# A transformer trunk in split fp32: the hi weight multiplies the hi and the lo half of an activation in one 512-column matmul, and the two partial sums are added when PSUM is read out

## The chip, the cores and the metric

The kernel runs on one core of one Trainium2 chip. The metric is device time in microseconds; three executions of the kernel before took 1297.39 to 1297.92 us, with a median of 1297.69 us.

## The reference

Two layers of a pre-norm residual network work on 256 tokens of width 1024 (float32), followed by a last RMSNorm. Cut to its matrix products, a layer is:

```python
# per layer; h is (256, 1024)
u = rms_norm(h, norm_mix_g)
q, k, v, g_ret, c_in, gates = split(u @ w_in)          # six parts: 1024, 1024, 2048, 2048, 2048, 2048 wide
y_a = (silu(g_ret) * group_norm(chunk_retention(rotary(q), rotary(k), v))) @ w_ret_out   # 2048 -> 1024
a, b = split(c_in)
y_b = silu(layer_norm(causal_dwconv(a * sigmoid(b), width=31))) @ w_conv_out + b_conv_out
g_a, g_b = split(sigmoid(gates + b_gate))
h = h + (g_a * y_a + g_b * y_b) @ w_mix_out
# cross-attention, 4 heads, into a memory of 256 tokens
kx, vx = split(rms_norm(mem, norm_mem_g) @ w_xkv)
h = h + softmax_attention(rms_norm(h, norm_xattn_g) @ w_xq, kx, vx) @ w_xo
# gated MLP, 1024 -> 2 x 2816 -> 1024
val, gate = split(rms_norm(h, norm_ffn_g) @ w_up)
h = h + (silu(causal_dwconv(gate, width=3)) * val) @ w_down
```

## The kernel before

**Split products.** Every weight and every activation of a projection is held as two tiles of the type fp32r: a hi part (a rounded copy) and a lo part (the value less its hi part). A product is the sum of three matmuls: hi weight on hi activation, hi weight on lo activation, lo weight on hi activation. The function `feat` (L166 to L174) issues these three for each 128 rows k of the contraction, with a 128x128 weight tile as the stationary operand and the 256 tokens as 256 moving columns. All three add up in the same 256 columns of a PSUM bank. `both` (L265) does the same for two output tiles in turn, so that the first k of both come before the last k of either. `tok` (L176) is the other way round, with the activation stationary and 512 weight columns moving, and serves the value and gate parts of the input projection and the values of the memory.

**Steps and weights.** The program is a list of steps, built in order by `mixer`, `cross` and `ffn` for each layer. Most steps are one chunk of 256 output features, that is two units of weights, one for each 128 features. `run` (L136) walks the list and, ahead of each step, emits the preparation of weight units up to four beyond those done (`UNITS`): `fetch` loads 1 MB by a DMA on SyncE's queue into one of four raw tiles, then `prepare` (L126) makes the hi part by a ScalarE copy (L131) and the lo part by a VectorE subtraction (L132). A list scheduler of the compiler orders each engine's instructions by priority and by when their inputs are ready; functions marked `urgent` (the residuals and the norms of h) have a higher priority.

**Buffers.** Activations of the size 1024 x 256 live in ten equal SBUF blocks (`BLOCKS`), which are handed out by whichever is free; a hi/lo pair takes two of them. Sums take a PSUM bank of 2 x 256 columns each; four such banks (tag `mm`) turn round for the projections, three (tag `att`) for attention, one (tag `nrm`) for norms. Small temporaries of 2 x 256 columns come from eight slots (`TEMPS`).

**Evictions.** What reads a projection's bank differs by stage: `split` (L161) writes hi on ScalarE (L163) and lo on VectorE (L164); `residual` (L334) adds the bank to h (L336), adds squares to the running sum of the next norm (`ssq_add`) and, where asked, writes an early copy of h times the norm's gain, split in hi and lo (`gained`, L252); conv_out adds a bias and multiplies by a gate (L704), then adds to the tile `m` (L708); the FFN's gate copies the bank on ScalarE first (L838), its value part multiplies out of the bank (L855).

**Order of the stages in a layer.** Input projection (conv parts, then per head queries, keys, values, gates, then the two mixing gates), ret_out (eight steps of 16 k each, L652), conv_out (four steps, L696), the first of four key steps of the memory (`mem_k`, L448), mix_out (four steps), three more key steps, during which h is normed for attention; then queries, attention with the values of the memory in between, xo (four steps, the first by `both`), the FFN's up projection in 22 steps and down projection in eight steps of 22 k each. The first four steps of the input projection and of the up projection run on the early copy (`ahead`, L293) while the norm's scale is worked out. The norm of the memory (`memory`, L434) loads the memory by a DMA on SyncE's queue (L438), sums its squares, and writes a normed hi/lo pair (`normed`, L321); it stands behind the seventh step of ret_out (`MEM_AT` = 6, L664). All matmuls are in TensorE's one queue, and so are the small matmuls that sum and spread a norm (L203, L211).

Of the kernel before, what the change touches and what calls it, by code (L numbers as in the profile page):

```python
# [13 lines left out]
P = 128  # L14
D = 1024
KT = 8
# [28 lines left out]
BLOCKS = 10  # L45
# [3 lines left out]
MEM_AT = 6  # L49


def by_token(x):
    return x.rearrange("p k n -> p (k n)").rearrange("p (t d) -> p t d", t=2)

# [9 lines left out]
class Trunk:  # L64
    def __init__(self, ctx, tc, io):
# [12 lines left out]
        self.background = []  # L78

# [4 lines left out]

    def block(self, dt=F32, tag="blk", bufs=BLOCKS):
        return self.bp.tile([P, KT, N], dt, name=self.nm(tag), tag=tag, bufs=bufs)
# [6 lines left out]

    def bank(self, tag="mm", bufs=4):
        return self.pp.tile([P, 2, N], F32, name=self.nm(tag), tag=tag, bufs=bufs)
# [79 lines left out]

    def tok(self, outs, ws, u, half):  # L176
# [13 lines left out]
    def flat_banks(self):  # L190
        return [self.bank().rearrange("p t n -> p (t n)") for _ in range(2)]
# [49 lines left out]
    def begin(self, gain=None):  # L241


        def fn():
            self.ssq, self.gain = None, gain
            if gain == "final":
                self.out = self.block()
            elif gain:
                self.early = self.block(F32R), self.block(F32R)
        self.step(fn)  # L250

    def gained(self, k, n):  # L252
# [68 lines left out]
    def normed(self, h, rstd, gname, layer):  # L321
        nc = self.nc
        uh, ul = self.block(F32R), self.block(F32R)
        for j in range(KT // 2):
# [5 lines left out]
            self.split(u, uh[:, 2 * j:2 * j + 2, :], ul[:, 2 * j:2 * j + 2, :])  # L330
        return uh, ul

    @urgent
    def residual(self, ps, k, n=2):  # L334
        h = self.h[:, k:k + n, :]
        self.nc.vector.tensor_tensor(h, ps, h, op=ALU.add)  # L336
# [97 lines left out]
    def memory(self, layer):  # L434
# [10 lines left out]
        self.xk = self.block(F32R), self.block(F32R)  # L445
        self.xv = self.block(F32R), self.block(F32R)

    def mem_k(self, layer, c, midway=None):  # L448
        def fn(*w):
            ps, pr = self.bank(), slice(2 * c, 2 * c + 2)  # L450
            self.each(ps, w, self.mem, midway)
            self.split(ps, self.xk[0][:, pr, :], self.xk[1][:, pr, :])
        self.step(fn, *self.pair("w_xkv", layer, c))

    def mem_v(self, layer, c):

        def fn(*w):
            if c % 2 == 0:
# [9 lines left out]
    def mixer(self, layer):  # L468
# [5 lines left out]
        def alloc_conv():  # L474
            X["c"], X["cc"] = self.block(), self.block()
# [95 lines left out]
        def gate(h):  # L571
# [5 lines left out]
            hi, lo = X["y"]  # L577
            b, r = h // 2, (h % 2) * 4
# [435 lines left out]
```

## Time and profile before

| What | Value |
|---|---|
| Median of three executions | 1297.69 us |
| Profiled execution, its own time | 1297.52 us |
| Its span, first to last instruction | 1295.7 us |
| Granted TensorE clock, mean | 0.997 |
| TensorE matmuls | 9632, busy 1278.4 us (99%) |
| VectorE | 1283 instructions, busy 972.8 us (75%) |
| ScalarE | 1365 instructions, busy 857.7 us (66%) |
| GpSimd | 31 instructions, busy 27.9 us (2%) |
| DMA | 227.32 MB, mean 175 GB/s |

A busy share is the part of the span in which an engine had an instruction in work. Matmuls overlap: the next starts before the last has ended, so the mean duration of one is a latency and the sum over a group is not a time that the group takes. PE in a row of the profile is TensorE's matmuls, PEld its loads of stationary operands, DVE is VectorE, ACT ScalarE, SP SyncE. A row's L number is a line of the kernel printed above. The idle time at a row's end is that of the engine ahead of the group's instructions, with what ended it behind an arrow.

### The profile page before, as it was taken

Reading aid. Unit: us, or ns where it says so; the run is one execution under the profiler, and the core shown is the slowest. Engines: PE = TensorE matmul, PEld = TensorE weight load, DVE = VectorE, ACT = ScalarE, POOL = GpSimd, SP = SyncE. Lnnn points to the kernel's source line nnn. Section 1 sums busy time; section 2 is a strip of 40 time slices with the busy share of each in tenths; the row PEclk is TensorE's granted clock in tenths of the full one; section 3 lists DMA queues with packets and bytes.
Section 4 is the critical chain, followed back from the end, with each engine's and each line's share of the span. In section 5 each row is a group of like instructions: output and inputs, shape, how many; then the busy total and the mean of one; then the engine's idle time right before and its main releaser. Section 6 shows DMA issues by size and latency. Waiting matters only on the chain.

```text
span 1295.7 us, 23296 instructions
## 1 busy us (share of the span) xinstructions
PE 1278.4 (99%) x9632; PEld 1225.2 (95%) x9632; DVE 972.8 (75%) x1283; ACT 857.7 (66%) x1365; POOL 27.9 (2%) x31
## 2 busy tenths in 40 slices
PE   7999999999999999999999999999999999999997
PEld 7998888999999999999999888899999989999997
DVE  8989998767676688665677999985686766876653
ACT  6899999664445557664469899986454554666542
POOL 0000000000000000000000010000000000000000
PEclk9999999999999999999999999999999999999998
DMA  8554444555554445544555444444654544455450
GB/s 306 208 180 163 163 158 169 193 187 194 178 190 137 157 168 192 190 163 181 189 190 183 170 158 172 163 165 162 228 190 172 176 147 163 169 189 189 156 178 33
DMA packets 33082, 227.32 MB, mean 175 GB/s; under 512 B 3920, under 2 KB 4176, under 8 KB 6736
## 3 DMA queue, kind: packets, MB, share of 16 engines
q1 hardware_dynamic: 32688, 225.32, 49.4%
q8 instruction: 75, 1.23, 0.4%
q10 hardware_dynamic: 288, 0.52, 0.1%
q14 instruction: 31, 0.25, 0.1%
HBM read 224.78 MB, written 1.05 MB: 174 GB/s over the span
## 4 chain that ended last, share of the span: by engine, by line
PE 84%; issue 14%; DMA 0%; DVE 0%; ACT 0%; SPq 0%; POOLq 0%; POOL 0%; DVEq 0%
PE mm L172 20%; PE mm L173 20%; PE mm L174 20%; PE mm L185 17%; PE mm L274 3%; PE att L553 1%; PE att L745 1%; PE att L746 1%; PE att L744 1%; PE att L575 1%; PE att L542 1%; PE att L555 1%; PE nrm L211 0%; DMA raw<-in_w_in_dram 0%; PE nrm L203 0%
## 5 line engine op out<-in xcount | busy, mean ns | idle before, releaser
L172 PE MATMUL mm<-blk,whi 128*128 128x256 f32 x2624 | 745.4, 285 | 0.0
L173 PE MATMUL mm<-blk,whi 128*128 128x256 f32 x2624 | 742.3, 283 | 0.0
L174 PE MATMUL mm<-blk,wlo 128*128 128x256 f32 x2624 | 742.2, 283 | 0.0
L131 ACT ACTIVATE whi<-raw 128x1024 fp32r<-128x1024 f32 (+1 forms) x424 | 443.2, 1050 | 346.4 <-PE mm L173 270.7
L132 DVE TENSOR_TENSOR wlo<-raw,whi 128x1024 fp32r<-128x1024 f32 (+1 forms) x424 | 511.0, 1211 | 193.8 <-ACT whi L131 191.9
L172 PEld LDWEIGHTS mm<-blk,whi 128*128 128x128 f32 x2624 | 502.8, 192 | 2.6 <-issue 1.7
L173 PEld LDWEIGHTS mm<-blk,whi 128*128 128x128 f32 x2624 | 503.0, 192 | 2.3 <-issue 2.2
L174 PEld LDWEIGHTS mm<-blk,wlo 128*128 128x128 f32 x2624 | 502.9, 192 | 0.3 <-issue 0.2
L185 PE MATMUL mm<-whi,blk 128*128 128x512 f32 x640 | 201.9, 391 | 0.0
L499 ACT ACTIVATE prod<-blk,params 128x255 f32<-128x255 f32 (+14 forms) x480 | 197.2, 487 | 3.8 <-DVE blk L502 3.8
L502 DVE TENSOR_TENSOR blk<-blk,prod 128x1020 f32<-128x1020 f32 (+14 forms) x120 | 138.2, 1151 | 7.9 <-ACT prod L499 6.8
L185 PEld LDWEIGHTS mm<-whi,blk 128*128 128x128 f32 x640 | 119.6, 188 | 25.1 <-issue 1.2
L185 PE MATMUL mm<-wlo,blk 128*128 128x512 f32 x320 | 128.2, 401 | 0.0
L185 PEld LDWEIGHTS mm<-wlo,blk 128*128 128x128 f32 x320 | 60.1, 188 | 12.8 <-issue 0.7
L163 ACT ACTIVATE blk<-t 128x512 fp32r<-128x512 f32 (+1 forms) x71 | 42.5, 614 | 16.1 <-DVE t L261 12.4
L164 DVE TENSOR_TENSOR blk<-t,blk 128x512 fp32r<-128x512 f32 (+1 forms) x71 | 47.0, 676 | 2.6 <-ACT blk L163 2.6
L274 PE MATMUL mm<-blk,whi 128*128 128x256 f32 x192 | 39.7, 295 | 7.9 <-ACT whi L131 7.9
L274 PEld LDWEIGHTS mm<-blk,whi 128*128 128x128 f32 x192 | 32.5, 201 | 7.9 <-ACT whi L131 7.9
L848 DVE SCALAR_TENSOR_TENSOR t<-t,params,t 128x255 f32<-128x255 f32 (+1 forms) x88 | 38.2, 478 | 0.0
L336 DVE TENSOR_TENSOR h<-mm,h 128x512 f32<-128x512 f32 (+1 forms) x26 | 16.9, 650 | 20.9 <-PE mm L174 16.0
L274 PE MATMUL mm<-blk,wlo 128*128 128x256 f32 x96 | 28.3, 295 | 1.1 <-DVE wlo L132 1.1
L218 POOL TENSOR_TENSOR rs_r<-rs_m,mhalf 128x2 f32<-128x2 f32 x11 | 8.5, 777 | 888.5 <-DVE rs_m L217 888.5
(133 smaller groups left out, 742.4 us busy)
## 6 DMA issues: line engine op xcount, KB each, us to landing
raw<-in_w_in_dram SPq DMA_DIRECT2D x79, 1024.0 KB, 4.9
raw<-in_w_up_dram SPq DMA_DIRECT2D x44, 1024.0 KB, 4.9
raw<-in_w_ret_out_dram SPq DMA_DIRECT2D x16, 1024.0 KB, 4.9
raw<-in_w_xkv_dram SPq DMA_DIRECT2D x16, 1024.0 KB, 4.9
raw<-in_w_down_dram SPq DMA_DIRECT2D x16, 1024.0 KB, 5.0
raw<-in_w_conv_out_dram SPq DMA_DIRECT2D x8, 1024.0 KB, 5.8
raw<-in_w_mix_out_dram SPq DMA_DIRECT2D x8, 1024.0 KB, 4.8
raw<-in_w_xq_dram SPq DMA_DIRECT2D x8, 1024.0 KB, 4.8
```

Of the source, the lines that this page charges most:

```text
L131: nc.scalar.activation(hi[:, :n], raw, AF.Copy)
L132: nc.vector.tensor_tensor(lo[:, :n], raw, hi[:, :n].bitcast(F32), op=ALU.subtract)
L163: self.nc.scalar.activation(hi, src, AF.Copy)
L164: self.nc.vector.tensor_tensor(lo, src, hi.bitcast(F32), op=ALU.subtract)
L172: self.nc.tensor.matmul(out, wh[:, k, :], uh[:, k0 + k, :], start=a, stop=False)
L173: self.nc.tensor.matmul(out, wh[:, k, :], ul[:, k0 + k, :], start=False, stop=False)
L174: self.nc.tensor.matmul(out, wl[:, k, :], uh[:, k0 + k, :], start=False, stop=b)
L185: mm = lambda a, b, p, q: self.nc.tensor.matmul(out, a[:, k, ts], b[:, j, :], start=p, stop=q)
L274: mm = lambda x, y, a, b: self.nc.tensor.matmul(out, x[:, k, :], y[:, k, :], start=a, stop=b, skip_group_check=True)
L499: nc.scalar.activation(t[:, i, :m], X["c"][:, k, :m], AF.Copy, scale=self.par("conv_dw_w", L, k * TAPS + TAPS - 1 - s))
L502: nc.vector.tensor_tensor(cc, cc, t[:, :, :m], op=ALU.add)
L848: nc.vector.scalar_tensor_tensor(g[:, f, s:], x[:, f, :N - s], wt(k, 2 - s), g[:, f, s:], op0=ALU.mult, op1=ALU.add)
```

## The change

A hi/lo pair becomes one tile with the two halves beside each other (`blocks`, `halved`, `Split`); there are five such pairs for the ten blocks. For every projection outside the input projection (and outside the first four up steps, which stay in `ahead`), `wide` streams hi and lo past the hi weight in one matmul of 2 x 256 columns, and then hi past the lo weight in one of 256 columns, which adds to the first 256. The 2 x 256 columns fill a bank, so a step with two output tiles takes two banks: `banks` hands out a pair of banks, of which there are two, and `bank` now hands out the halves of such a pair in turn. `add_up` copies the second sums to SBUF on ScalarE and adds the first on VectorE; `residual` adds both to h one after the other. `gained` writes the hi half by a scaled ScalarE copy and the lo half by one fused VectorE operation. The first xo step no longer uses `both`. In ret_out the product with the gate is written over the gate, and the tile `m` is gone. `memory` moves from behind the seventh step of ret_out to behind the first step of conv_out, and the tiles for the memory's values, for attention's output and for the FFN's activations are taken only where they are first written.

```diff
-BLOCKS = 10
+BLOCKS = 5
-MEM_AT = 6
+MEM_AT = 0
+    def blocks(self, dt=F32):
+        return self.bp.tile([P, 2, KT, N], dt, name=self.nm("blk"), tag="blk", bufs=BLOCKS)
+    def banks(self):
+        self.spare = None
+        return self.pp.tile([P, 2, 2, N], F32, name=self.nm("mm"), tag="mm", bufs=2)
...
+    def wide(self, ps, w, u, first=True, last=True):
+        kt = w[0].shape[1]
+        for k in range(kt):
+            self.nc.tensor.matmul(ps, w[0][:, k, :], u.tile[:, :, k, :], start=first and k == 0, stop=False)
+            self.nc.tensor.matmul(ps[:, 0, :], w[1][:, k, :], u[0][:, k, :], start=False, stop=last and k == kt - 1)
+
+    def wides(self, w, u):
+        pair = self.banks()
+        for f, x in enumerate(w):
+            self.wide(pair[:, f], x, u)
+        return pair
+
+    def add_up(self, pair):
+        t = self.temp()
+        self.nc.scalar.activation(t, pair[:, :, 1, :], AF.Copy)
+        self.nc.vector.tensor_tensor(t, pair[:, :, 0, :], t, op=ALU.add)
+        return t
...
-            t, pr = self.temp(), slice(k, k + n)
-            for i in range(n):
-                nc.vector.tensor_scalar(t[:, i, :], self.h[:, k + i, :], self.par(*self.gain, k + i), None,
-                                        op0=ALU.mult)
-            self.split(t[:, :n, :], self.early[0][:, pr, :], self.early[1][:, pr, :])
+            for i in range(k, k + n):
+                hi, lo = (x[:, i, :] for x in self.early)
+                g = self.par(*self.gain, i)
+                nc.scalar.activation(hi, self.h[:, i, :], AF.Copy, scale=g)
+                nc.vector.scalar_tensor_tensor(lo, self.h[:, i, :], g, hi.bitcast(F32), op0=ALU.mult,
+                                               op1=ALU.subtract)
...
-        self.nc.vector.tensor_tensor(h, ps, h, op=ALU.add)
+        for j in range(2):
+            self.nc.vector.tensor_tensor(h, pair[:, :, j, :], h, op=ALU.add)
...
-            self.each(ps, w, self.mem, midway)
-            self.split(ps, self.xk[0][:, pr, :], self.xk[1][:, pr, :])
+            for f in range(2):
+                self.wide(pair[:, f], w[f], self.mem)
+                if midway and f == 0:
+                    midway()
+            self.split(self.add_up(pair), self.xk[0][:, pr, :], self.xk[1][:, pr, :])
...
-            if f == MEM_AT:
-                self.step(lambda: self.memory(L))
...
             self.step(fn, *self.pair("w_conv_out", L, j))
+            if j == MEM_AT:
+                self.step(lambda: self.memory(L))
...
-                ps = self.bank()
-                (self.each if j else self.both)(ps, w, X["o"])
-                self.residual(ps, 2 * j)
+                self.residual(self.wides(w, X["o"]), 2 * j)
...
-                    self.feat(X["ps"][:, at, :], w[b], X["a"][b], first=b == 0, last=b == 2)
+                    self.wide(X["ps"][:, f % 2], w[b], X["a"][b], first=b == 0, last=b == 2)
```

More of the change, by code (lines that the diff above doesn't have):

```diff
@@ L83, in nm, with block, halved @@
         return f"{s}_{self.uid}"
-    def block(self, dt=F32, tag="blk", bufs=BLOCKS):
-        return self.bp.tile([P, KT, N], dt, name=self.nm(tag), tag=tag, bufs=bufs)
+    def blocks(self, dt=F32):
+        return self.bp.tile([P, 2, KT, N], dt, name=self.nm("blk"), tag="blk", bufs=BLOCKS)
+    def block(self):
+        return self.blocks()[:, 0]
+    def halved(self):
+        return Split(self.blocks(F32R))
     def small(self, shape, tag, dt=F32, bufs=2):
@@ L190, in flat_banks @@
     def flat_banks(self):
-        return [self.bank().rearrange("p t n -> p (t n)") for _ in range(2)]
+        pair = self.banks()
+        return [pair[:, t].rearrange("p t n -> p (t n)") for t in range(2)]
     def halves(self, x):
@@ L248, in fn @@
             elif gain:
-                self.early = self.block(F32R), self.block(F32R)
+                self.early = self.halved()
         self.step(fn)
@@ L474, in alloc_conv @@
         def alloc_conv():
-            X["c"], X["cc"] = self.block(), self.block()
+            t = self.blocks()
+            X["c"], X["cc"] = t[:, 0], t[:, 1]
         def start():
@@ L631, in alloc_gates @@
         def alloc_gates():
-            X["gt"] = (self.block(), self.block())
+            t = self.blocks()
+            X["gt"] = t[:, 0], t[:, 1]
         self.step(alloc_gates)
@@ L823, in start @@
             X["u"] = self.normalise("norm_ffn_g", L, keep=True)
-            X["a"] = [(self.block(F32R), self.block(F32R)) for _ in range(3)]
+            X["a"] = []
         ahead = []
```

97 lines of the change are left out of this document (46 added, 51 removed).

## The prediction

> **What bounds the kernel now.** I read the page first (shares of busy time, the 40 slices, the costliest groups), then the chain of waits, then the timeline for the distance between two matmuls, then busy time by stage, and last the timeline of VectorE at the places where the change adds work. In the page, a group's line ends with its busy time, the mean of one in ns, and the idle time before it.
>
> ```profile
> span 1295.7 us, 23296 instructions
> PE 1278.4 (99%) x9632; PEld 1225.2 (95%) x9632; DVE 972.8 (75%) x1283; ACT 857.7 (66%) x1365; POOL 27.9 (2%) x31
> PE   7999999999999999999999999999999999999997
> DVE  8989998767676688665677999985686766876653
> PEclk9999999999999999999999999999999999999998
> PE 84%; issue 14%; DMA 0%; DVE 0%; ACT 0%; SPq 0%; POOLq 0%; POOL 0%; DVEq 0%
> L172 PE MATMUL mm<-blk,whi 128*128 128x256 f32 x2624 | 745.4, 285 | 0.0
> L173 PE MATMUL mm<-blk,whi 128*128 128x256 f32 x2624 | 742.3, 283 | 0.0
> L174 PE MATMUL mm<-blk,wlo 128*128 128x256 f32 x2624 | 742.2, 283 | 0.0
> ```
>
> TensorE is busy in every slice, almost all of the traced chain is TensorE or time in which nothing was waited for, and the three matmul lines of the feature projection show no idle time before them. VectorE is at 75%, ScalarE at 66%. So the length of TensorE's instruction stream sets the time, and a matmul costs its distance to the next one, not its 283 ns of latency. That distance is in the timeline (start, length) and in the chain (start, length, what):
>
> ```profile
> 1005.08 0.28 PE L172 MATMUL mm<-blk,whi 128*128 128x256 f32 x1
> ...
> 1011.92 0.28 PE L172 MATMUL mm<-blk,whi 128*128 128x256 f32 x1
> ```
> ```profile
> 743.95 0.12 PE mm L174
> 744.07 10.91 PE mm L185 x48
> ```
>
> Between the two first rows lie 57 matmuls of 256 columns: 6.84 / 57 = 120.0 ns each. The 48 matmuls of 512 columns took 10.91 / 48 = 227.3 ns each; a 256-column one in front of them still took 0.12 us. So 256 more columns cost 107.3 ns, and each matmul carries 120.0 - 107.3 = 12.7 ns that don't depend on its columns.
>
> **The change, part by part.** *The wide matmul.* Three matmuls of 256 columns (hi weight on hi, hi weight on lo, lo weight on hi: L172 to L174) become one of 512 and one of 256: 3 x 120.0 = 360.0 ns against 227.3 + 120.0 = 347.3 ns, 12.7 ns less. The same columns stream; one start is gone. How often, per layer: ret_out 8 x 16 = 128, conv_out, mix_out, xq, xo and the key half of xkv 64 each = 320, w_up outside the first four steps 18 x 16 = 288, w_down 8 x 22 = 176: 912, in two layers 1824. That fits the page: 2624 groups now, of which 2 x (23 + 3) x 16 = 832 stay at L172 to L174, and 32 of the removed come from L274. 1824 x 12.7 ns = **-23.2 us**.
>
> The Trainium skill (TensorE: Matmul & The Clock Gate, Back-to-back issue gap) puts a warm gap at N/2.4 + 2.5 ns. By that the start is worth 2.5 ns and the removal 1824 x 2.5 = 4.6 us; the rows above have 12.7 ns, and I go by them.
>
> Not in the trace is a moving operand in two runs of 256 columns that lie 2048 elements apart. From below, the jump costs nothing (a gain is excluded: the columns stream at 107.3 ns per 256 either way); from above, as much as the start it replaces, 12.7 ns, which would undo the part. I take 0, the nearest row being the 512-column matmul, which differs in nothing but the jump.
>
> *The sum at eviction.* Each of 68 steps gets a ScalarE copy and a VectorE add (18 gate steps had the copy already, L838), each of the 26 residuals a second VectorE add. The rows for them, by form, then busy time by stage (window, its length, each engine's busy time):
>
> ```profile
> L838 ACT ACTIVATE t<-mm 128x512 f32<-128x512 f32 x18 | 10.5, 582 | 0.0
> L336 DVE TENSOR_TENSOR h<-mm,h 128x512 f32<-128x512 f32 x22 | 15.2, 691 | 12.6 <-PE mm L174 7.7 <-PE mm L274 4.8
> ```
> ```profile
> 306.40:329.50 23.10, 23.10 (x194) 23.10 (x194) 20.53 (x30) 11.27 (x14) 0.00 (x0) 1.00 0.50 171
> 434.00:457.00 23.00, 23.00 (x194) 23.00 (x194) 16.32 (x25) 11.65 (x15) 0.00 (x0) 1.00 0.46 159
> 516.00:585.00 69.00, 69.00 (x578) 69.00 (x576) 46.75 (x60) 41.49 (x55) 0.00 (x0) 1.00 0.50 179
> ```
>
> 0.58 us on ScalarE and 0.69 on VectorE, hidden if the engines keep up. The FFN stretch (516 to 585) is six pairs of steps of 11.5 us with 7.8 us of VectorE each; with two more adds 9.2 of 11.1 us, 83%, and ScalarE 7.5 of 11.1. Output projection of attention (434 to 457): 16.3 / 4 = 4.1 us of VectorE per step, with the add 4.8 of 5.56 us (the early copy for the next norm, where ScalarE takes over a multiply, only takes work off VectorE). Cost 0, hidden under matmuls; with that cover gone it would be 1.27 us at each of 114 wide steps' ends.
>
> *Two pairs of PSUM banks for four banks.* A step may begin when the pair of the step before last is read out. After a step ends, its copy may stand behind one weight conversion on ScalarE (L131, 1.06) and its add behind one on VectorE (L132, 1.22): 1.06 + 0.58 + 1.22 + 0.69 = 3.5 us, and 5.56 are there. Cost 0.
>
> ```profile
> L131 ACT ACTIVATE whi<-raw 128x1024 fp32r<-128x1024 f32 x408 | 429.6, 1058 | 321.3 <-PE mm L173 247.7 <-issue 29.9 <-PE mm L274 17.9
> L132 DVE TENSOR_TENSOR wlo<-raw,whi 128x1024 fp32r<-128x1024 f32 x408 | 495.7, 1221 | 174.6 <-ACT whi L131 172.7
> ```
>
> *The memory norm, moved from the seventh of eight ret_out steps to behind the first conv_out step.* What moves: one 1 MB load on SyncE's queue, four squares on ScalarE, VectorE's sums, eight TensorE matmuls of the norm with GpSimd's power between them, then eight fused multiplies and four splits. Five matmul steps stood between it and the first key step, which reads its result; now three do. VectorE, timeline:
>
> ```profile
> 288.38 1.49 DVE L231 TENSOR_TENSOR t<-t,t 128x512 f32<-128x512 f32 x2 [0.77 <-ACT t L224]
> 290.99 0.69 DVE L231 TENSOR_TENSOR t<-t,t 128x512 f32<-128x512 f32 x1
> 291.71 0.43 DVE L195 TENSOR_TENSOR t<-t 128x256 f32<-128x256 f32 x1
> 304.04 3.22 DVE L328 SCALAR_TENSOR_TENSOR t<-blk,params,nrm 128x256 f32<-128x256 f32 x8 [2.03 <-PE nrm L211]
> ```
> ```profile
> 282.42 0.33 SPq L438 DMA_DIRECT2D blk<-in_mem_dram  x1
> ```
>
> Conv_out (306.4 to 329.5) is the stage in which VectorE is tightest, 20.5 of 23.1 us. After: 22.2 us of matmuls, and 20.5 + 4 x 0.69 (adds) + 3.2 (the multiplies, now inside) = 26.5 us; with the sums too (1.49 + 0.69 + 0.43 = 2.6) 29.1 us. Over by 4.3 to 6.9 us a layer. Against it stand four converted weight units ahead of TensorE, 4 x 1.22 = 4.9 us of VectorE's work that may be late, and made good in the key and mix_out steps behind. So the stall is 0 from below (the load is issued as soon as a block is free, as now at 282.42, long before the norm's multiplies at 304.04, and the sums stay ahead: 4.3 < 4.9) and 6.9 from above (no lead left). Between, 6.9 - 4.9 = 2.0; I take 1.0 per layer, **+2.0 us**. What is late next is the first key step; behind the norm on VectorE stand the adds of conv_out, for which TensorE's pair waits. The two norm matmuls sit in TensorE's queue in front of conv_out's matmuls.
>
> *The norm ahead of attention.* Its VectorE work already fills the time until the query steps:
>
> ```profile
> 369.50 3.22 DVE L328 SCALAR_TENSOR_TENSOR t<-h,params,nrm 128x256 f32<-128x256 f32 x8
> 372.63 1.22 DVE L132 TENSOR_TENSOR wlo<-raw,whi 128x1024 fp32r<-128x1024 f32 x1
> 373.77 0.69 DVE L164 TENSOR_TENSOR blk<-mm,blk 128x512 fp32r<-128x512 f32 x1
> 374.37 2.48 DVE L164 TENSOR_TENSOR blk<-t,blk 128x512 fp32r<-128x512 f32 x4
> ```
>
> From 369.50 to 376.85 it has no idle time, and two key steps now bring an add of 0.69 each: 0 to 1.4 us a layer; I take 0.5, **+1.0 us**.
>
> *The end.* The last residual does two adds of one tile in a row:
>
> ```profile
> 1284.86 0.42 DVE L336 TENSOR_TENSOR h<-mm,h 128x256 f32<-128x256 f32 x1 [7.49 <-PE mm L174]
> ```
>
> **+0.4 us**, with nothing over it. Dropping the interleaved order of both weight halves in the first xo step, the blocks taken as pairs, and the first split at the start are 0: the matmuls of the other half stay free to run while the last head is late; if not, six of eight k of that half, 6 x 0.347 = 2.1 us a layer.
>
> *Sum*, against the profiled execution's own 1297.5 us (span 1295.7 and 1.8 around it; the median of the runs shown is 0.2 higher): 1297.5 - 23.2 + 2.0 + 1.0 + 0.4 = **1277.7 us**.
>
> **The rivals.** *VectorE becomes the bound in conv_out.* For it: 26.5 to 29.1 us of work in 22.2. Against: the lead of four units, and the 1.00 share of TensorE in every stage now, also where VectorE is at 93% (186.5 of 200 us):
>
> ```profile
> 24.00:224.00 200.00, 200.00 (x1253) 178.00 (x1252) 186.53 (x253) 184.66 (x352) 10.27 (x8) 1.00 0.50 173
> ```
>
> Price: the full 6.9 and 1.4 us in both layers, 1297.5 - 23.2 + 16.6 + 0.4 = 1291.3, or from 1283 on where part of it comes.
>
> *The jump in the moving operand costs a start.* Place: every one of the 1824 wide matmuls; price 12.7 ns; then nothing is saved and the stalls remain: 1297.5 + 3.4 = 1300.9, slower. It decides from 19.8 us / 1824 = 10.9 ns on. For it: no row has such an operand. Against: 107.3 ns per 256 columns leaves no sign of a bound on reading.
>
> *The pairs come free too late throughout.* Place: the start of every wide step. If two more conversions stand ahead on either engine, 3.5 + 2 x 1.22 = 5.9 us against 5.56, 0.4 us at each of 114 steps = 46 us: about 1323. It decides at 19.8 / 114 = 0.17 us a step. Against it: one unit is converted per 2.8 us of matmuls, so two rarely queue. The Trainium skill (Perfetto Trace Analysis, Optimization Strategy) reads a gap that repeats as a sign of too little PSUM for the next tile; the present trace has none.
>
> *A start is worth little.* If 10.2 of the 12.7 ns came back at the change between wide and narrow, 2.5 x 1824 = 4.6 us would be saved and 3.4 lost: 1296.3. Against: 0.12 us stands before the row of 512 columns unchanged. This is the time by the gap that the Trainium skill's page on TensorE gives, cited above.
>
> **How the numbers follow.** Forecast 0.66 (its own range 1273 to 1283), VectorE in conv_out 0.20, the jump 0.07, the pairs 0.04, little per start 0.03. About 0.2% is what a measurement of this kernel can tell from no change. Faster: 0.66 + 0.20 = 0.86; same 0.03; slower 0.11. The range runs from 1272.5 (no stall at all: 1274.7, and 2 us less for 1 ns more per wide matmul than I read) to 1290, which takes in nearly all of the VectorE case.
>
> **What would show it.** Right: TensorE matmuls 1824 fewer; in the FFN stretch a pair of wide and narrow every 347 ns; no idle time before the wide lines; a TensorE share near 99%. The jump would show as more than 227 ns behind each wide matmul, the pairs as an idle time at the same place in each step with an eviction as its releaser, the VectorE case as idle TensorE at the end of conv_out and before the first key step, released by VectorE's weight half, add or split. Wrong altogether would be the whole argument if TensorE's share fell below 97%.

## The result, and the profile after

The changed kernel takes 1374.88 us (median of 4 runs, 1372.79 to 1379.95) against 1297.7 before: 1.0601 times as long by the mean times, 95% interval 1.0571 to 1.0630. It is 77 us slower where 20 us faster was forecast.

From the page of the kernel after (shares, slices, chain, and two groups with busy time, mean of one in ns, idle time before them and what ended most of it):

```profile
span 1372.5 us, 19854 instructions
PE 1289.6 (94%) x7808; PEld 1140.1 (83%) x7808; DVE 1029.0 (75%) x1360; ACT 886.0 (65%) x1430; POOL 27.3 (2%) x31
PE   6899999998799998999999999999969999999997
PEclk9999999999899999999999999999979999999998
PE 70%; issue 16%; DVE 9%; ACT 4%; POOL 1%; DMA 1%; SPq 0%; DVEq 0%; POOLq 0%; ACTq 0%
L209 PE MATMUL mm<-blk,whi 128*128 128x512 f32 x1824 | 653.5, 402 | 31.1 <-DVE blk L192 15.8
L200 PE MATMUL mm<-blk,whi 128*128 128x256 f32 x832 | 239.6, 289 | 10.2 <-DVE t L341 8.5
```

The 1824 matmuls are gone (9632 before, 7808 now), and yet TensorE is busy for longer: 1289.6 us against 1278.4. Its share fell from 99% to 94%, below the 97% that the prediction named as the mark of a wrong argument. Span less busy time is 82.9 us now and was 17.3. So of the 77 us of span, 65.6 are waiting, and TensorE's busy time has grown by 11.2 although there are fewer matmuls.

Waits of TensorE, before and then after (who waits for what: us in all, times, longest):

```profile
PE mm L274 <- ACT whi L131: 7.9, 1, 7.9
PE nrm L211 <- POOL rs_r L218: 1.1, 1, 1.1
```
```profile
PE mm L209 <- DVE blk L192: 15.8, 4, 6.0
PE mm L209 <- DVE t L222: 9.6, 4, 4.0
PE mm L325 <- ACT whi L159: 8.8, 1, 8.8
PE mm L200 <- DVE t L341: 8.5, 4, 7.1
PE nrm L253 <- DVE t L245: 8.4, 2, 4.2
```

Before, TensorE waited at the start and at the end only. After, it waits in the middle, mostly for VectorE: for the low half of a split that a new stage reads (L192: the convolution's output z, and the norm ahead of attention), for a sum at eviction (L222), for the eviction of the early steps (L341, `scaled`), for the memory's sum of squares (L245). All stand at the start of a stage, and most come once per layer. VectorE's share has not changed (75%): it isn't full, its work comes late.

The longest one in a stage's middle, at the start of conv_out, by windows of TensorE (window, its length, busy time and matmuls, granted clock, DMA share, GB/s):

```profile
318.00:321.00 3.00, 3.00 (x19) 1.00 0.63 188
321.00:327.30 6.30, 0.29 (x3) 0.77 0.18 77
327.30:331.00 3.70, 3.70 (x11) 0.50 0.41 126
331.00:334.00 3.00, 3.00 (x18) 0.96 0.46 194
```

TensorE waits 6 us for z, and for 3.7 us behind that it has the half clock: 11 matmuls where some 21 would have gone. Such stretches make the busy time longer (the mean granted clock is 0.979, and was 0.997); this one adds about 1.9 us to its wait.

What the wide matmul itself did, from the timeline of the kernel after, the first and the last row of a stretch in which 424 pairs of wide and narrow stand without a break:

```profile
531.38 0.40 PE L209 MATMUL mm<-blk,whi 128*128 128x512 f32 x1
...
681.20 0.40 PE L209 MATMUL mm<-blk,whi 128*128 128x512 f32 x1
```

149.82 / 424 = 353.3 ns a pair: 6.7 ns less than the three narrow ones took (360.0), not 12.7.

The memory's load went out at 282.42 before; in the kernel after it goes out 55 us later, behind the end of ret_out (SyncE's queue):

```profile
337.60 0.42 SPq L490 DMA_DIRECT2D blk<-in_mem_dram  x1
```

### The profile page after: what moved, and what is told of

It reads as the page before. It is cut to its first block, busy times and chain, and to the rows that moved or that the text cites. A ratio compares the mean times of both kernels' runs of the same rounds, so it can differ in the third digit from the quotient of the medians.

```text
span 1372.5 us, 19854 instructions
## 1 busy us (share of the span) xinstructions
PE 1289.6 (94%) x7808; PEld 1140.1 (83%) x7808; DVE 1029.0 (75%) x1360; ACT 886.0 (65%) x1430; POOL 27.3 (2%) x31
## 4 chain that ended last, share of the span: by engine, by line
PE 70%; issue 16%; DVE 9%; ACT 4%; POOL 1%; DMA 1%; SPq 0%; DVEq 0%; POOLq 0%; ACTq 0%
PE mm L209 22%; PE mm L234 14%; PE mm L210 11%; PE mm L200 5%; PE mm L202 5%; PE mm L201 5%; DVE wlo L160 3%; DVE t L379 2%; ACT whi L159 1%; DVE blk L559 1%; PE mm L325 1%; DVE blk L192 1%; PE att L610 1%; ACT prod L556 1%; PE att L789 1%
## 5 line engine op out<-in xcount | busy, mean ns | idle before, releaser
L209 PE MATMUL mm<-blk,whi 128*128 128x512 f32 x1824 | 653.5, 402 | 31.1 <-DVE blk L192 15.8
L210 PE MATMUL mm<-blk,wlo 128*128 128x256 f32 x1824 | 516.6, 283 | 2.3 <-DVE wlo L160 2.3
L209 PEld LDWEIGHTS mm<-blk,whi 128*128 128x128 f32 x1824 | 346.7, 190 | 117.5 <-issue 29.2
L210 PEld LDWEIGHTS mm<-blk,wlo 128*128 128x128 f32 x1824 | 348.8, 191 | 3.0 <-DVE wlo L160 3.0
L200 PE MATMUL mm<-blk,whi 128*128 128x256 f32 x832 | 239.6, 289 | 10.2 <-DVE t L341 8.5
L202 PE MATMUL mm<-blk,wlo 128*128 128x256 f32 x832 | 235.1, 284 | 1.2 <-DVE wlo L160 1.2
L201 PE MATMUL mm<-blk,whi 128*128 128x256 f32 x832 | 235.9, 284 | 0.0
L234 PE MATMUL mm<-whi,blk 128*128 128x512 f32 x640 | 205.7, 396 | 2.2 <-ACT whi L159 2.2
L200 PEld LDWEIGHTS mm<-blk,whi 128*128 128x128 f32 x832 | 160.1, 193 | 15.2 <-issue 8.9
L201 PEld LDWEIGHTS mm<-blk,whi 128*128 128x128 f32 x832 | 160.2, 193 | 2.2 <-issue 1.7
L202 PEld LDWEIGHTS mm<-blk,wlo 128*128 128x128 f32 x832 | 159.7, 193 | 1.6 <-DVE wlo L160 1.6
L191 ACT ACTIVATE blk<-t 128x512 fp32r<-128x512 f32 x62 | 37.0, 624 | 14.4 <-DVE t L379 8.1
L222 DVE TENSOR_TENSOR t<-mm,t 128x512 f32<-128x512 f32 x68 | 46.3, 683 | 0.0
L388 DVE TENSOR_TENSOR h<-mm,h 128x512 f32<-128x512 f32 (+1 forms) x52 | 33.6, 647 | 15.1 <-PE mm L210 14.5
L192 DVE TENSOR_TENSOR blk<-t,blk 128x512 fp32r<-128x512 f32 x62 | 40.9, 682 | 1.6 <-ACT blk L191 1.3
```

The source lines that it names most:

```text
L192: self.nc.vector.tensor_tensor(lo, src, hi.bitcast(F32), op=ALU.subtract)
L200: self.nc.tensor.matmul(out, wh[:, k, :], uh[:, k0 + k, :], start=a, stop=False)
L201: self.nc.tensor.matmul(out, wh[:, k, :], ul[:, k0 + k, :], start=False, stop=False)
L202: self.nc.tensor.matmul(out, wl[:, k, :], uh[:, k0 + k, :], start=False, stop=b)
L209: self.nc.tensor.matmul(ps, w[0][:, k, :], u.tile[:, :, k, :], start=first and k == 0, stop=False)
L210: self.nc.tensor.matmul(ps[:, 0, :], w[1][:, k, :], u[0][:, k, :], start=False, stop=last and k == kt - 1)
```

## The experiments

All times are medians. Each ratio is one of mean times, to the kernel before run beside it on the same chip; its medians there were 1297.5 to 1297.9 us. Kernels in different groups of experiments ran on different chips.

| kernel | edit, and of what | us | ratio, 95% interval |
|---|---|---|---|
| b_halves | before, banks as halves of two-bank tiles | 1374.67 | 1.0592 [1.0576, 1.0607] |
| a_own_sums | after, own slots for the sums | 1373.13 | 1.0580 [1.0562, 1.0598] |
| a_side_by_side | after, hi and lo of a k adjacent | 1375.00 | 1.0595 [1.0554, 1.0637] |
| after_narrow | after, wide as two narrow | 1373.37 | 1.0576 [1.0559, 1.0594] |
| a_banks | after, four single banks | 1335.03 | 1.0285 [1.0270, 1.0300] |
| a_banks_sums | a_banks, own slots for the sums | 1320.35 | 1.0167 [1.0152, 1.0182] |
| a_tags | a_banks_sums, own slots for single blocks | 1302.82 | 1.0043 [1.0028, 1.0059] |
| a_tags6 | a_tags, memory norm at its old place | 1295.06 | 0.9978 [0.9969, 0.9987] |
| a_mix | a_tags6, memory keys narrow | 1292.03 | 0.9957 [0.9940, 0.9974] |
| a_mix3 | computes and orders as a_mix | 1290.84 | 0.9947 [0.9932, 0.9962] |
| a_up2 | a_mix, third up step narrow | 1288.03 | 0.9923 [0.9910, 0.9935] |
| a_up3 | a_up2, fourth up step narrow | 1287.91 | 0.9925 [0.9911, 0.9939] |
| a_narrow | a_mix, wide as two narrow | 1305.59 | 1.0059 [1.0044, 1.0074] |
| a_up2_halves | a_up2, banks as halves again | 1361.03 | 1.0488 [1.0474, 1.0503] |

**Which part of the change costs.** The theory was that four banks handed out as halves of two tiles make TensorE wait, the rivals that the convolution's norm comes late by its slots, or that the jump in the moving operand costs.

b_halves takes the kernel before and changes nothing but where its banks come from:

```diff
+    def banks(self):
+        self.spare = None
+        return self.pp.tile([P, 2, 2, N], F32, name=self.nm("mm"), tag="mm", bufs=2)
     def bank(self, tag="mm", bufs=4):
...
-        return self.pp.tile([P, 2, N], F32, name=self.nm(tag), tag=tag, bufs=bufs)
+        if self.spare is None:
+            pair = self.banks()
+            self.spare = pair[:, 1]
+            return pair[:, 0]
+        mine, self.spare = self.spare, None
+        return mine
```

> The kernel before with one edit: PSUM banks are handed out as the two halves of a two-bank tile, two such tiles in turn, as in the changed kernel; no wide matmul, no sum at eviction, blocks as before. Theory (the second half of a two-bank tile waits until the first half is read out, although they are different banks): the input projection and the steps on the early copy lose what they lost in the changed kernel, about 13 to 17 us a layer, 7 us at the start and some us in the up projection: 1325 to 1340 us, with the steps of TensorE's order interleaved there. Rival (the halves cost nothing, the loss is from the wide matmul and its evictions): 1297 to 1300 us.

Measured: 1374.67 us, 76.9 more than before. There is no wide matmul in it, no sum at eviction and no moved norm, and it is as slow as the whole change. One place in the second half of an FFN (w_down), from its timeline:

```profile
640.35 0.28 PE L186 MATMUL mm<-blk,wlo 128*128 128x256 f32 x1
...
640.66 0.69 DVE L349 TENSOR_TENSOR h<-mm,h 128x512 f32<-128x512 f32 x1 [0.44 <-PE mm L186]
...
641.50 0.35 PE L184 MATMUL mm<-blk,whi 128*128 128x256 f32 x1 [0.88 <-DVE h L349]
```

At 640.35 the first half of a tile gets its last matmul; L349 reads it from 640.66 to 641.35; only then does the next matmul start, though it writes the other half, another bank. The two halves are one tile, and a write to one waits for the reads of the other. The next such read, at 657.60, belongs by the order in which `bank` hands halves out to a tile's second half, and TensorE goes on beside it without a break; after the third, at 673.44, it waits 0.88 us again. With four single tiles this line has no idle time before it (L172, 0.0, in the page of before). The time from b_halves is above both the theory's 1340 and its rival's 1300: the mechanism is there, its price was set too low. One more cost is inside that price: `banks` gives up a spare half when it is asked for a whole pair. No run separates it from the waits.

a_own_sums leaves the banks and takes the sums at eviction out of the slots that all temporaries share (those of one kind are handed out in the order of the program, so that the convolution's norm stood behind ret_out's sums):

```diff
-TEMPS = 8
+TEMPS = 6
...
-        t = self.temp()
+        t = self.sp.tile([P, 2, N], F32, name=self.nm("ts"), tag="ts", bufs=2)
```

> The changed kernel, with the sums of add_up in two slots of their own and six slots for the other temporaries, in place of eight for both. Theory (slots of one kind are given out in program order, so the norm of the conv branch, which comes behind the first ret_out eviction in the program, can't run ahead of it): the norm runs some 50 us earlier, during the gate steps; the 6.2 us stall ahead of conv_out goes, in both layers: 1355 to 1364 us. Rival (the norm is late because VectorE or TensorE is late): unchanged, 1370 to 1378 us, with the norm at its present place.

Measured: 1373.13 us, no change that can be told. The norm did come early, the 6 us wait at conv_out went, and other waits took its place: 5.8 us twice behind the gates. While the halves are tied, mending one norm brings nothing.

a_side_by_side lays hi and lo of each k next to each other, so that the wide matmul reads one run of 512:

```diff
-        self = super().__new__(cls, (tile[:, 0], tile[:, 1]))
+        self = super().__new__(cls, (tile[:, :, 0, :], tile[:, :, 1, :]))
...
-... u.tile[:, :, k, :] ...
+... u.tile[:, k] ...
```

> The changed kernel, with hi and lo of the same k beside each other in the tile, so that the 512 moving columns lie in one run; the memory's values keep the old layout. Theory (the 235 ns behind a wide matmul in place of 227 are the jump between the halves): 227 ns behind it and 344 to 347 ns per pair, up to 8 ns x 1824 = 14 us less: 1360 to 1368 us. Rival (the 235 ns come with the switch from 512 to 256 columns, or with the halves of PSUM they write): 235 ns still, 1371 to 1378 us.

Measured: 1375.00 us, the same. The time alone couldn't settle it, since in this kernel time saved in matmuls is waited for again (after_narrow, below). The trace does: without the jump, the same 424 pairs go at 346.7 ns in layer 0 (531.85 to 678.83) and at 353.3 in layer 1 (1199.97 to 1349.77), and with the jump both paces occur too (last section). The jump isn't the cause.

a_banks undoes the tie in the kernel after. A wide step takes two single banks, and each is evicted by itself, by instructions of 256 columns:

```diff
-        return self.pp.tile([P, 2, 2, N], F32, name=self.nm("mm"), tag="mm", bufs=2)
+        return [self.bank(), self.bank()]
...
-        self.nc.scalar.activation(t, pair[:, :, 1, :], AF.Copy)
-        self.nc.vector.tensor_tensor(t, pair[:, :, 0, :], t, op=ALU.add)
+        for f, ps in enumerate(pair):
+            self.nc.scalar.activation(t[:, f, :], ps[:, 1, :], AF.Copy)
+            self.nc.vector.tensor_tensor(t[:, f, :], ps[:, 0, :], t[:, f, :], op=ALU.add)
```

> The changed kernel with four single-bank tiles in place of two two-bank tiles; a wide step takes two of them and reads out each by itself (two copies and two adds of 256 columns, four adds for a residual). Theory (two-bank tiles tie the halves together): the input projection takes the time of before, the start loses its 7 us, the last down step no longer waits for the residual ahead of it: 30 to 45 us less, 1330 to 1345 us. Rival (the loss is the rotation of two pairs or the evictions' length): no gain or slower by the extra evictions, 1370 to 1385 us.

Measured: 1335.03 us, 40 us less than after, as expected, and still 37 above before. What TensorE waits for now, in its view of waits:

```profile
PE mm L201 <- DVE t L334: 9.4, 2, 4.7
PE nrm L246 <- DVE t L238: 8.4, 2, 4.2
PE mm L201 <- DVE blk L184: 8.4, 4, 2.2
PE mm L201 <- DVE t L215: 7.5, 2, 3.7
```

Places that come once per layer: the up steps behind the early ones (L334), the memory's norm (L238) and the steps behind it (L215), the norms ahead of conv_out and of attention (L184). These were taken one after the other.

**The late norms.** a_banks_sums gives the sums their own slots (the diff of a_own_sums, now on a_banks).

> As a_banks, and the sums at eviction get two slots of their own (TEMPS 8 to 6), so that the convolution's norm is no longer placed behind the output steps of retention by its slots. Theory (stalls at the ends of stages, each with a stretch of half clock behind it, now make up the difference): the 2.1 us in which TensorE waits for z at the start of conv_out goes, in both layers, with what follows it at half clock: 4 to 8 us less than a_banks' 1335.0, so 1327 to 1331. Rival (the stall only moves to the next late norm, as it did in a_own_sums): 1333 to 1338, with the memory's norm waiting longer.

Measured: 1320.35 us, 14.7 less, some twice the 4 to 8 that were expected. The line that adds two halves of a square sum, first in a_banks, then in a_banks_sums (durations, first and last start in layer 0; x2 are the convolution's two sums, x1 the memory's):

```profile
L238 DVE TENSOR_TENSOR t<-prod x2: 418/418/419, 265.6 to 283.3; 128x256 f32<-128x256 f32 x2
L238 DVE TENSOR_TENSOR t<-t x1: 426/426/426, 331.1 to 331.1; 128x256 f32<-128x256 f32 x1
```
```profile
L238 DVE TENSOR_TENSOR t<-prod x2: 421/422/423, 243.8 to 261.3; 128x256 f32<-128x256 f32 x2
L238 DVE TENSOR_TENSOR t<-t x1: 418/418/418, 327.7 to 327.7; 128x256 f32<-128x256 f32 x1
```

The convolution's norm is 22 us earlier and the wait at conv_out is gone; the memory's is still at 327.7.

a_tags gives the blocks that aren't split pairs two slots of their own, so that the memory gets one that the convolution's input frees, and not one that ret_out still reads:

```diff
-BLOCKS = 5
+BLOCKS = 4
...
     def block(self):
-        return self.blocks()[:, 0]
+        return self.bp.tile([P, KT, N], F32, name=self.nm("one"), tag="one", bufs=2)
...
-            t = self.blocks()
-            X["c"], X["cc"] = t[:, 0], t[:, 1]
+            X["c"], X["cc"] = self.block(), self.block()
```

> As a_banks_sums, and blocks that are not split pairs (the convolution's input and output, the output block) get two single slots of their own, with four pairs beside them; the block that takes the memory comes out of a pair. Theory (the memory comes late because its block is only handed out when the output of retention has been read, 55 us later than before; the three waits of its norm and first steps, 4.4, 1.3 and 4.1 us in a_banks, and the half clock behind them are then gone): 1327 less about 2 x (9.7 + 3) = 1302 to 1312. Rival (the memory's norm is late because conv_out's evictions fill VectorE, whatever its block): the waits stay at 8 us or more a layer and the time at 1325 to 1335.

a_tags6 also puts the memory's norm back behind the seventh ret_out step (`MEM_AT = 6`, called in ret_out's loop).

> As a_tags, and the memory's norm stands behind the seventh output step of retention, where it stood before the change, and not behind the first step of conv_out. Theory (place and block both make the norm late): 2 to 10 us under a_tags, 1297 to 1308. Rival (with the block free early enough the place costs nothing): within 2 us of a_tags.

Measured: a_tags 1302.82 us, as expected, and a_tags6 1295.06, another 7.8 less: inside the 2 to 10 us that were expected, though below the 1297 that was given as the range's end. In a_tags the memory's load goes out at 258.88, and the sum of its squares is at 270.9 instead of 327.7:

```profile
258.88 0.33 SPq L484 DMA_DIRECT2D one<-in_mem_dram  x1
```
```profile
L238 DVE TENSOR_TENSOR t<-t x1: 419/419/419, 270.9 to 270.9; 128x256 f32<-128x256 f32 x1
```

In a_tags6 both stand where they stand in a_tags (258.47 and 270.5). So the memory was late by its block alone, and that was worth 17.5 us. The 7.8 us of its place show as a later norm ahead of attention. The four splits of the memory's norm run at 317.8 to 320.7 in a_tags, among the evictions of conv_out, where VectorE has no idle time from 315.8 to 334.7; in a_tags6 they run at 305.4 to 307.9. The last split that mix_out reads starts 3.2 us later, and TensorE's wait for the norm ahead of attention is 5.3 us in each layer instead of 2.5, with more half clock behind it. The last split and that wait, in a_tags and then in a_tags6, where waits of 2 us and more are left at two places behind the start:

```profile
336.70 0.68 DVE L184 TENSOR_TENSOR blk<-blk,blk 128x512 fp32r<-128x512 f32 x1
```
```profile
PE mm L201 <- DVE blk L184: 10.7, 2, 5.3
```
```profile
333.50 0.68 DVE L184 TENSOR_TENSOR blk<-blk,blk 128x512 fp32r<-128x512 f32 x1
```
```profile
PE mm L201 <- DVE t L334: 5.0, 4, 2.1
PE mm L201 <- DVE blk L184: 5.0, 2, 2.5
```

a_tags6 is 0.2% faster than before.

a_mix was meant to go back to 256 columns at both places:

```diff
-            self.split(self.add_up(pair), self.xk[0][:, pr, :], self.xk[1][:, pr, :])
+            ps, pr = self.bank(), slice(2 * c, 2 * c + 2)
+            self.each(ps, w, self.mem, midway)
+            self.split(ps, self.xk[0][:, pr, :], self.xk[1][:, pr, :])
...
+            def up(w, j=j):
+                if j > 2:
+                    return self.add_up(self.wides(w, X["u"]))
+                ps = self.bank()
+                self.each(ps, w, X["u"])
+                return ps
```

> As a_tags6, and the steps that need banks or a norm early go with 256 columns again, all of them: the four steps of memory keys in each layer (96 wide instructions less in a layer) and the third up step, gate and value (32 less); the rest stays wide. Theory (a wide pair is worth about 8 ns; a wait at a stage's start is worth 2 to 5 us and the clock behind it): the 4.8 us wait of the first up step after the four early ones and most of the 2.4 us of the norm ahead of attention go in both layers, against 2 x 128 x 8 ns = 2 us given back: 8 to 15 us under a_tags6, 1285 to 1297, which would be no slower than before the change. Rival (wide matmuls cost more in eviction than they bring, wherever they stand): over 1300.

Measured: 1292.03 us, 3.0 less. Only half of the edit took effect. The page counts 7936 matmuls, 128 more than after, and those are the memory keys (64 wide ones a layer, not 96 as the expectation says). The function `up` is looked up when a step runs, when the loop has long ended, so that every up step stayed wide. What a_mix shows is the keys: with them narrow the wait for the norm ahead of attention is gone in one layer and shorter in the other:

```profile
PE mm L201 <- DVE blk L184: 1.7, 1, 1.7
```

**What the wide matmul is worth by itself.** a_narrow and after_narrow split the 512-column matmul of a_mix and of after into two of 256 into the same bank, and keep all else:

```diff
-            self.nc.tensor.matmul(ps, w[0][:, k, :], u.tile[:, :, k, :], start=first and k == 0, stop=False)
-            self.nc.tensor.matmul(ps[:, 0, :], w[1][:, k, :], u[0][:, k, :], start=False, stop=last and k == kt - 1)
+            mm(0, w[0], u[0], a, False)
+            mm(1, w[0], u[1], False, False)
+            mm(0, w[1], u[0], False, b)
```

> As a_mix, but in each wide step the 512-column matmul is two of 256 columns into the two halves of the same bank (hi past the high half, hi past the low half, lo past the high half: the same products into the same sums, the same banks, the same evictions; only 1696 instructions more). It prices the wide matmul alone. Theory (the wide pair goes at a median of 350 ns where three narrow ones take 360): 1696 x 8 to 10.5 ns = 14 to 18 us more than a_mix, 1306 to 1310. My forecast's 12.7 ns would give 1313 to 1314. Rival (what a_mix won came from order and places, not from the wide matmuls): under 1298.

> The kernel after, with the same edit: the wide matmul as two of 256 columns, everything else of the change kept. Theory (the wide matmul helps there too, but part of the columns' time it saves is waited for again, since the stalls end with evictions and norms that come when they come): 8 to 18 us more than after, 1383 to 1393. Rival (faster matmuls only lengthen the stalls): 1373 to 1378, no different from after.

Measured: a_narrow 1305.59 us, 13.6 more than a_mix: 13.6 / 1696 = 8.0 ns per wide pair. Against a_mix3, which issues the same instructions as a_mix and ran on a_narrow's chip, it is 14.8 us and 8.7 ns. after_narrow 1373.37 us, where after took 1374.88: no difference. From the pages of a_mix and then a_narrow, and the group of after_narrow that answers to L209 above:

```profile
span 1290.2 us, 20274 instructions
PE 1264.7 (98%) x7936; PEld 1133.3 (88%) x7936; DVE 1029.1 (80%) x1456; ACT 880.6 (68%) x1482; POOL 31.3 (2%) x31
```
```profile
span 1303.4 us, 23659 instructions
PE 1280.6 (98%) x9632; PEld 1226.8 (94%) x9632; DVE 1027.9 (79%) x1456; ACT 880.2 (68%) x1482; POOL 28.2 (2%) x31
```
```profile
L210 PE MATMUL mm<-blk,whi 128*128 128x256 f32 x3648 | 666.7, 285 | 17.0 <-DVE t L226 9.1 <-DVE t L345 3.3 <-DVE blk L192 2.5
```

Where TensorE never waits, time saved in matmuls is time saved. In the kernel after it is waited for again: idle time before the first matmul of a wide pair is 17.0 us with narrow ones and 31.1 with wide ones, the difference almost all behind L192 (2.5 against 15.8).

a_mix3 was meant to make the fourth up step narrow as well.

> As a_mix, and the fourth up step (gate and value) goes with 256 columns too. Theory (the 2.2 us wait behind the early up steps is the first wide step asking for two banks at once, and goes): 2 x (2.3 + 1.5 at half clock) less 2 x 32 x 10 ns = 0.6: 1285 to 1289. Rival (the wait is for the late norm of the early steps, and moves or stays): 1291 to 1293.

For the reason told above its up steps stayed wide too; it is a_mix over again, 1290.84 us, and shows how far two medians of one program lie apart here: 1.2 us.

**The up steps in earnest, and the price of the tie.** a_up2 and a_up3 hand the step's number over (`up(w, j)`), so that the third, or the third and fourth, up step is narrow. a_up2_halves puts the two-bank tiles back under a_up2 and keeps the eviction half by half:

```diff
-        return [self.bank(), self.bank()]
+        self.spare = None
+        pair = self.pp.tile([P, 2, 2, N], F32, name=self.nm("mm"), tag="mm", bufs=2)
+        return [pair[:, 0], pair[:, 1]]
```

> As a_mix, and the third up step (gate and value), the first behind the four early ones, really goes with 256 columns: 64 matmuls more, 8000. In a_mix and a_mix3 the up steps had stayed wide. Theory (the wait of 2.2 us and the 0.5 us ahead of it are a wide step's need of two free banks while the early steps hold four): both are gone in both layers, 2 x 2.7 less 64 x 8 ns = 0.5: about 5 us under the 1290.8 to 1292.0 of a_mix3 and a_mix, 1286 to 1288. Rival (the early steps are read out too late for one bank as well): the wait stays, 1291 to 1293.

> As a_up2, and the fourth up step too: 8064 matmuls. Theory: nothing further to win, 0.5 us more than a_up2, 1286 to 1289. Rival (the two-bank wait of the first wide step moves one step on): it is a_up2 that still waits, and a_up3 is 3 to 5 us under it.

> As a_up2, but the four banks are again the halves of two two-bank tiles; evictions still go half by half, and everything else stays. Theory (the two halves wait for each other's readers, wherever they stand): 40 us (what single banks brought in the kernel after) to 77 us (what halves cost the kernel before) over a_up2, 1326 to 1365. Rival (the halves only cost where they also turned the order of stages over): within 15 us of a_up2.

Measured: a_up2 1288.03 us, a_up3 1287.91, a_up2_halves 1361.03. The wait behind the early up steps was a wide step's need of two free banks while the early ones hold four, and one narrow step cures it: of the 5.0 us behind L334 in a_mix, 1.1 are left in a_up2. A second one (a_up3) brings nothing more. The first two rows are a_up2's page; the others a_up2_halves', its last two from the waits:

```profile
span 1286.3 us, 20392 instructions
PE 1265.0 (98%) x8000; PEld 1136.1 (88%) x8000; DVE 1026.3 (80%) x1448; ACT 878.6 (68%) x1474; POOL 31.4 (2%) x31
```
```profile
span 1358.0 us, 20424 instructions
PE 1290.0 (95%) x8000; PEld 1149.3 (85%) x8000; DVE 1031.5 (76%) x1448; ACT 884.2 (65%) x1476; POOL 27.1 (2%) x31
...
PE mm L201 <- DVE t L343: 20.1, 4, 6.9
PE mm L210 <- DVE blk L193: 10.6, 6, 3.4
```

The tie costs 73 us in an order of work that otherwise runs almost without waits: 46.7 us more idle TensorE (68.0 against 21.3) and 25.0 us more busy time for the same 8000 matmuls, at a mean granted clock of 0.985 against 0.998. The largest item, 20.1 us, stands where early steps hold their banks: the free half of a tile can't be written until `scaled` (L343) has read the held half. How much of the rest is direct waiting for the other half and how much follows from the order that these waits bring about, or from spare halves given up, these runs don't separate.

a_up2 keeps the wide matmul in 1632 of 1824 places and is 0.77% faster than before (0.65 to 0.90): 9.5 us, of the 20 that were forecast.

## Why the prediction was wrong

**The step that failed: "Two pairs of PSUM banks for four banks … Cost 0".** It asked whether a wide step finds its pair free, 3.5 us of eviction against 5.56, and it looked at wide steps alone. But the same edit makes `bank` hand out halves to every narrow step, in the input projection and the early steps too, and makes two banks one tile. Of two steps that share a tile, the second then waits for the read of the step just before it, not of the one before last. This part, set at 0, measured +76.9 us by itself (b_halves), +73.0 in a good order (a_up2_halves), and taking it out of the change brought 39.9 (a_banks). The rival "the pairs come free too late throughout", at 0.04 and 1323 us, was nearest. It saw the pair rule, but put the place at the 114 wide steps and the cause in queued conversions, so its price was 46 us. (Its 114 is 1824 / 16; by the forecast's own count of 68 sums and 26 residuals the program reads out wide steps 94 times.)

**The terms that were mis-sized or missing.** The ladder from after to a_up2 prices them, each on top of the ones ahead of it, both layers together.

- *Wide matmul, -23.2 us*: the mechanism is right (1824 matmuls less, the same columns), the size is not: 8.0 to 8.7 ns a pair by a_narrow instead of 12.7, so 14.6 to 15.9 us for all 1824. The 2.5 ns of the rival "a start is worth little", 4.6 us in all, are ruled out by the same run. In the kernel after none of the saving reaches the end.
- *Memory norm, +2.0 us*: 7.8 for its place (a_tags to a_tags6). By the order in the trace the mechanism is the one that the working and the VectorE rival named, too much VectorE work in conv_out, though no run tests it by itself; the wait stands elsewhere, not at the first key step but at the norm ahead of attention.
- *Blocks as pairs, 0*: 17.5 (a_tags). The working took the load "issued as soon as a block is free, as now at 282.42". With blocks handed out as pairs the next one is free only when ret_out has been read; the load went out at 337.60. In a_tags, with the norm's place unchanged, it goes out at 258.88, and the waits behind L238 and L215 are gone.
- *The sums at eviction, cost 0*: 14.7 (a_banks_sums). Their own 0.58 and 0.69 us are hidden, as said. Their slots are not free: they come out of the eight that the convolution's norm uses, and push it behind ret_out. The forecast never counted slots.
- *The norm ahead of attention, +1.0 us*: about 3 to 4 (a_mix and a_mix3 against a_tags6, with what half clock followed), the right mechanism.
- *Early up steps*: not in the forecast. About 3 to 4 (a_mix3 and a_mix to a_up2): four held banks and a step that wants two.

**What held.** *The jump in the moving operand* costs nothing that the traces show (a_side_by_side). The sign that the forecast named for it, more than 227 ns behind a wide matmul, did appear (353.3 less 117 for the narrow one is 236), but it appears without the jump too, in layer 1 of a_side_by_side. *The FFN stretch* is bound by matmuls alone, as forecast: 424 pairs without a break, at 353.3 ns and not at 347. *The end*, +0.4, wasn't tested by itself.

**What no term could hold.** Every duration was taken at full clock. A longer wait can be followed by half clock, so a late norm can cost more than its wait. Of the 71.7 us between the spans of a_up2 and a_up2_halves, 25.0 are busy time. The granted clock can account for at most (0.998 - 0.985) x 1358 = 17.7 us of them; where the rest comes from stays open.

## What to carry to other kernels

Before a change of buffers is costed at nothing, list every user of that kind of buffer, not only the step that the change is about, and ask of each what must be read before it may write: banks joined into one tile are also joined in their waits, and slots of one kind bind whatever takes them in the order of the program. In a kernel at 99% of its bound engine, time taken off that engine only counts where the work behind it has slack; a norm or a load that was just in time becomes the wait. A saving per instruction is best measured by splitting the instruction again with everything else kept.

## What the runs showed of the hardware

**The clock.** Two waits of 2.5 us stand at one place in the two layers of a_tags6, the norm ahead of attention. Behind the first TensorE ran at half clock for 2.9 us, behind the second it did not. From windows of TensorE, layer 0 and then layer 1:

```profile
373.40:376.10 2.70, 0.20 (x3) 0.91 0.20 85
376.10:379.00 2.90, 2.90 (x9) 0.50 0.00 0
```
```profile
1009.20:1011.80 2.60, 0.13 (x2) 1.00 0.17 72
1011.80:1014.50 2.70, 2.67 (x15) 1.00 0.03 6
```

So the length of a wait alone does not decide it here.

The Trainium skill (TensorE: Matmul & The Clock Gate, What's actually happening) puts the fall to half rate behind an idle window of about 3.4 us, and the way back behind a busy one as long. The return agrees (2.9 and 3.7 us here); the fall came after shorter waits, 2.5 us in the first pair of rows.

**Two paces for one instruction stream.** In a_up2 the 147 pairs of w_down that follow without a break go at one pace in layer 0 and at another in layer 1 (first and last start of each; the next row would be another line's):

```profile
591.85 0.40 PE L201 MATMUL mm<-blk,whi 128*128 128x512 f32 x1
...
642.47 0.40 PE L201 MATMUL mm<-blk,whi 128*128 128x512 f32 x1
...
1223.63 0.40 PE L201 MATMUL mm<-blk,whi 128*128 128x512 f32 x1
...
1275.22 0.40 PE L201 MATMUL mm<-blk,whi 128*128 128x512 f32 x1
```

From first to last lie 146 pairs: 50.62 / 146 = 346.7 ns and 51.59 / 146 = 353.4 ns, at full clock in both. Code, shapes and weights' layout are the same. Nor is it the layer: a_mix and a_mix3 issue the same instructions, and the same 147 pairs of layer 0 go at 353.4 ns in one (594.29 to 645.88) and at 346.6 in the other (591.89 to 642.50). What sets the pace stays open. The forecast's 347.3 is the faster one, and the kernel after ran both its FFN stretches at the slower. Against 360.0 the two paces save 13.3 and 6.7 ns a pair, and the 8.0 to 8.7 that a_narrow shows lie between them. No row of the kernel before could show it: its triples go at 360.0 throughout.
